# A hybrid encoder block: the sixth products' weights of two more halves summed by VectorE, turned gate rows stored and turned at other steps

## The chip, the core and the metric

The kernel runs on one core of a Trainium2 chip. Four engines compute: TensorE multiplies matrices (PE in the profile; PEld is its loading of weights), VectorE (DVE) and ScalarE (ACT) work on elements, GpSimd (POOL) here mostly issues DMA transfers. SyncE (SP) issues most of the others. Sixteen DMA engines carry all transfers of the core. The metric is the time of one execution in microseconds (us), the median of several runs; lower is better.

## The reference

One encoder layer on a sequence of 256 tokens of width 2048, all in float32. What matters here is that nearly all its work is products of the normalised input with wide weight matrices, and that some columns of `w_in` are gates:

```python
xn = rms_norm(x, norm_pre_w[l])
z = xn @ w_in[l]                    # 2048 x 13312
u_lru, g_lru, q, k, v, g_attn, m_lru, m_attn = jnp.split(z, split_at, axis=-1)
...
y_a = h.astype(x.dtype) * jax.nn.silu(g_lru)
...
y_b = windowed_gqa(q, k, v, attn_sink[l]) * jax.nn.silu(g_attn)
merged = (jax.nn.sigmoid(m_lru) * (y_a @ w_proj_a[l])
          + jax.nn.sigmoid(m_attn) * (y_b @ w_proj_b[l]))
x = x + rms_norm(merged @ w_out[l], norm_post_w[l])
```

## The kernel before

**Weights in two parts.** TensorE multiplies in a reduced float format (float32r), so every weight tile is split into a high part, rounded by a cast on ScalarE (line 222), and a low part, the rest, subtracted on VectorE (line 224). TensorE then multiplies high and low parts (lines 256, 258, 278, 435). Each 1 MB of weights passes as two halves, so ScalarE and VectorE have one instruction of 128 x 1024 elements each for every half.

**Steps and ticks.** The order of all weight pieces is written out by hand in START, MERGE and OUT. A step is one piece: a "block" (128 columns, two ticks long; blocks come in pairs), a "quad" (two ticks), or a "part" (one tick) of a group that saves a product. `soon(f, d)` calls f d ticks later, `at(n, f)` at tick n, in the order of the program; each engine runs its own instructions in that order. `seconds` lists the ticks at which the second block of a pair begins. Weights are fetched three steps ahead into a ring of three buffers (`raw`), high parts are made two steps ahead, low parts one and a half.

**Groups of seven.** L, H, M, N, A and O each compute a 1024-column product by seven products instead of eight (class `Seven`). Their names in START are, for example, Hm3.1: group H, third product, second half of the rows. L, H, M and N are the halves that lie in START, the first stage; H is half of the attention gate, the others are merge gates. The left operands are sums of input blocks, and the right operands are sums of weight blocks that build up in cells: x holds W11, then adds the second block (m5), then the third (m6), then the fourth (m4); y holds W for m3, then adds one for m7. Cells have the names Hx0a, Hx0b, Hx1a, Hx1b (group, cell, row half, a or b) and the like for y. Each addition is a DMA that reads weights from memory and adds them to the cell (`load(..., add=True)`, line 195, issued by POOL; queue q0 software_dynamic). It can go out when the cell's former content has been split by ScalarE and VectorE. `Seven.fetch` issues it five steps ahead, unless the group's products stand in ADDED (line 68). In that case `split` adds the third product's cell y to x on VectorE right behind the low part of the third product (line 227), since the weights that the sixth product needs added are those that m3 has alone. Before the change N, A and O do so for m6.

**Turned gate rows.** Group H yields rows of the attention gate with tokens on partitions, four tiles of 128 x 512 (`hr`). `silu_rows` applies the sigmoid and the product, and later `turn` transposes them on TensorE (line 831, into a PSUM buffer `ht` of a pool of two, which blocks in pairs use too), copies the result back with ScalarE (line 832), and `store` writes it to memory (`parksga`, line 839, on SP's queue), 256 KB each. A turn is put at the first second block that begins more than two ticks behind the sigmoid.

**Buffers.** Nearly everything big lives in one pool of 45 buffers of 4 KB a partition (`units`): high and low parts, cells, gate rows, input, LRU tiles, tiles on their way to memory and back. A new tile takes the buffer that has been free the longest, and its first writer waits until the former tile's last reader is done, a DMA store among them. Tiles that leave early go to memory by `park` (line 863; `parkq` is a tile of queries, `parkya` one of the LRU branch).

Of the kernel before, what the change touches and what calls it, by code (L numbers as in the profile page):

```python
# [64 lines left out]
LRU = (-4, 0, 0, 0, 0, 0, 0, 0)  # L65
QUADS = {"u": ("w_in", U0), "v": ("w_in", V0), "p": ("w_proj_a", 0),
         "b": ("w_proj_b", 0), "o": ("w_out", 0)}
ADDED = {'A': {'m3': 'm6', 'm2': 'm4'}, 'O': {'m3': 'm6'}, 'N': {'m3': 'm6'}}
PAIRS = {"g": GL0, "h": GA0, "w": U0, "k": K0, "q": Q0}
SEVENS = {"L": ("w_in", ML0 + 1024), "M": ("w_in", ML0), "N": ("w_in", MA0), "A": ("w_in", MA0 + 1536), "H": ("w_in", GA0 + 1024), "O": ("w_out", 0)}  # L70

# [39 lines left out]
def body(ctx, tc, x, x0, xT, wall, wlru, pvec, npost, ident_d, mask_d, rope_d, out):  # L111
# [9 lines left out]
    def unit(name, dt=F32, shape=(P, 4, S)):  # L121
        return units.tile(list(shape), dt, tag="u", name=name)
# [4 lines left out]
    def banks(name, shape=(P, 2, 2, S)):  # L127
        return psum.tile(list(shape), F32, tag="mm", name=name, bufs=2)

    def half_unit(name, tag, dt=F32, bufs=2):  # L130
        return small.tile([P, 2, S], dt, tag=tag, name=name, bufs=bufs)
# [20 lines left out]
    now = [0]  # L152

    def ticks(i=None):
        return sum(1 if p[0] == "part" else 2 for p in plan[:len(steps) if i is None else i])

    def at(hs, fn):
        assert hs >= now[0], (hs, now[0])
        due.setdefault(hs, []).append(fn)
# [9 lines left out]
    seconds, hs, n = [], 0, 0  # L169
# [7 lines left out]
    def soon(fn, d=1):  # L177
        at(now[0] + d, fn)
# [11 lines left out]
    def load(cell, p, add=False):  # L190

        w = wall[row[content(p)]]
        for h in range(2):
            if add:
                nc.gpsimd.dma_start(flat(cell[h]), w[:, h * 1024:(h + 1) * 1024], accum_op=ALU.add)
            else:
                nc.sync.dma_start(flat(cell[h]), w[:, h * 1024:(h + 1) * 1024])
# [14 lines left out]
    def split(q, c=0, w=1024, cast=nc.scalar.copy, only=None):  # L212
# [10 lines left out]
        if only != "h":  # L223
            nc.vector.tensor_tensor(ls, raw, hs.bitcast(F32), ALU.subtract)  # L224
            if plan[i][0] == "part" and plan[i][2] in ADDED.get(plan[i][1], ()):
                x = flat(groups[plan[i][1]].cells["x", plan[i][3]][h])
# [137 lines left out]
    def x_sum(name, s, q):  # L364
        t = unit(name, F32R, (P, 4, 2, P))
        nc.sync.dma_start(t.rearrange("p a b c -> p a (b c)").bitcast(F32), away[q][:, SUMS.index(s)])
        return t

    class Seven:
# [22 lines left out]
        def fetch(self, p, lead):  # L392
            m, q = p[2:]
            fresh = ("m1", "m3") if self.sums is None else ()
            if self.sums is None:
                if lead == 4 and m in fresh:
                    self.start(self.where(m), q)
                if lead == 4 and SEVEN[m][0][0] == "s" and self.name in "NA":
                    self.kept[m, q] = x_sum(f"{self.name}{m}{q}", SEVEN[m][0], q)
            if lead == 5 and m in ("m5", "m6", "m7", "m4")[self.sums is not None:] and m not in ADDED.get(self.name, {}).values():  # L400
                load(self.cell(m, q), p, True)
# [394 lines left out]
    def combine(to, ps, other, sign):  # L796
        nc.vector.scalar_tensor_tensor(to, ps, float(sign), other, ALU.mult, ALU.add if sign > 0 else ALU.subtract)
# [17 lines left out]
    def silu_rows(g):  # L815

        def done(t, c, ps, other, sign):
            u = unit(f"hr{g}{c}{t}")
            f, y = flat(u)[:, 0:512], u[:, 2:4].rearrange("p a (b s) -> p (a b) s", b=2)
            rt = rtok[:, t:t + 1]  # L820

            def sigmoid(src):
                sg = flat(half_unit(f"hs{c}{t}", "p"))
                nc.scalar.activation(sg, src, AF.Sigmoid, scale=rt)
                soon(lambda: nc.vector.scalar_tensor_tensor(f, src, rt, sg, ALU.mult, ALU.mult))
                at(min(b for b in seconds if b > now[0] + 2), turn)

            def turn():
                pt = banks(f"ht{c}{t}", (P, 4, P))
                for j in range(4):  # L830
                    nc.tensor.transpose(pt[:, j], f[:, j * P:(j + 1) * P], ident)
                nc.scalar.copy(y, pt)
                soon(store, 5)

            def store():
                key = "sga", g + c
                if key not in parked:
                    parked[key] = dram.tile([P, 1024], F32, name=f"parksga{g + c}")
                nc.sync.dma_start(parked[key].rearrange("p (j s) -> p j s", j=4)[:, :, t * P:(t + 1) * P], y)

            if other is None:
                sigmoid(ps)
            else:
                combine(f, ps, other, sign)
                soon(lambda: sigmoid(f))
        return done
# [317 lines left out]
    b, n = ticks(), ticks(len(plan))  # L1164
# [159 lines left out]
```

## Time and profile before

| | |
|---|---|
| median of 3 runs | 885.68 us (883.79 to 886.96) |
| the profiled execution | 884.68 us, span 882.9 us |
| granted TensorE clock, mean | 0.996 |
| busy: PE, DVE, ACT | 862.4, 750.3, 657.3 us |
| DMA | 244.77 MB, mean 277 GB/s |
| group H on TensorE | about 248 to 358 us of the span |
| group M on TensorE | about 357 to 460 us |

How to read the lines below. Rows of waits are "engine, line, tile waited for: us in total, times, longest". Rows of the chain of waits are "start us, us, what". Rows of the timeline are "start us, us, engine, line, operation, out<-in, count", with the engine's idle time before it in brackets and what ended it. Rows of groups are "line, engine, operation, tiles, count: duration in ns min/median/max, first and last start". Rows of windows give, for a stretch of the span, busy us and instructions of PE, PEld, DVE, ACT, POOL, then the granted TensorE clock, the busy share of the DMA engines and GB/s. Rows of DMA issues are "out<-in, queue, operation, count, KB each, median us from issue to landing". L224 is line 224 of the kernel.

### The profile page before, as it was taken

To read this page: it belongs to the slowest core of one execution; us is meant where nothing else is said; L and a number is where in the kernel's file an instruction comes from. 1 tells how busy PE (TensorE), PEld (TensorE's weight loads), DVE (VectorE), ACT (ScalarE), POOL (GpSimd) and SP (SyncE) were. 2 spreads that over 40 slices of the span, in tenths; PEclk is the share of its full clock that TensorE was granted. 3 is DMA by queue.
4 is the path that set the end of the run, shared out by engine and by line. 5 is a ranking of instruction groups with operands and counts; after the bars stand their busy time and mean duration, and the time that the engine had idled before them with its cause. 6 is when DMAs were issued, how large, how long until landed. Compare 5 with 4: busy or idle time off the path is not lost.

```text
span 882.9 us, 12249 instructions
## 1 busy us (share of the span) xinstructions
PE 862.4 (98%) x4378; PEld 733.9 (83%) x4378; DVE 750.3 (85%) x999; ACT 657.3 (74%) x939; POOL 73.0 (8%) x105
## 2 busy tenths in 40 slices
PE   9999999999999979999999999999999999999996
PEld 8888888888888868788888888778888888788885
DVE  6998999898898869797897887897669778998886
ACT  7689698969879868987976779996558545665654
POOL 0000001022011200112100020000000100000200
PEclk9999999999999999999999999999999999999999
DMA  9757699999999985999989998798999987988982
GB/s 328 275 191 250 196 315 290 278 298 250 306 255 350 260 206 195 293 270 295 280 270 328 305 288 301 251 324 334 272 327 370 298 325 215 309 311 316 266 205 95
DMA packets 68045, 244.77 MB, mean 277 GB/s; under 512 B 6416, under 2 KB 24592, under 8 KB 53264
## 3 DMA queue, kind: packets, MB, share of 16 engines
q1 hardware_dynamic: 52480, 198.37, 61.4%
q0 software_dynamic: 11520, 41.95, 25.1%
q10 hardware_dynamic: 3984, 3.67, 1.3%
q8 instruction: 34, 0.56, 0.2%
q14 instruction: 27, 0.22, 0.1%
HBM read 223.52 MB, written 20.45 MB: 276 GB/s over the span
## 4 chain that ended last, share of the span: by engine, by line
PE 81%; DMA 5%; DVE 5%; issue 4%; ACT 2%; SPq 1%; ACTq 1%; POOLq 0%; DVEq 0%
PE q L258 6%; PE gl L258 6%; PE u L258 5%; PE Lm L435 4%; PE Nm L435 4%; PE Hm L435 4%; PE Am L435 3%; PE ga L258 3%; PE q L256 3%; PE gl L256 3%; PE Om L435 3%; PE Mm L435 3%; PE pb__7297 L278 2%; PE pa__5741 L278 2%; PE pa__5992 L278 2%
## 5 line engine op out<-in xcount | busy, mean ns | idle before, releaser
L224 DVE TENSOR_TENSOR wl<-raw,wh 128x1024 fp32r<-128x1024 f32 (+1 forms) x240 | 285.2, 1201 | 53.1 <-ACT wh L222 38.6
L222 ACT CAST wh<-raw 128x1024 fp32r<-128x1024 f32 (+1 forms) x239 | 241.1, 1035 | 60.9 <-DMA raw<-wall_dram 31.1
L258 PE MATMUL gl<-xs,wh 128*128 128x512 f32 x256 | 64.8, 397 | 0.0
L258 PE MATMUL q<-xs,wh 128*128 128x512 f32 x256 | 63.9, 392 | 0.0
L258 PEld LDWEIGHTS gl<-xs,wh 128*128 128x128 f32 x256 | 48.1, 193 | 9.4
L258 PEld LDWEIGHTS q<-xs,wh 128*128 128x128 f32 x256 | 46.8, 188 | 9.0
L258 PE MATMUL u<-xs,wh 128*128 128x512 f32 x192 | 47.6, 391 | 0.0
L258 PEld LDWEIGHTS u<-xs,wh 128*128 128x128 f32 x192 | 35.1, 188 | 6.7
L256 PE MATMUL gl<-xs,wl 128*128 128x256 f32 x256 | 34.3, 285 | 5.1 <-DVE wl L224 5.1
L256 PEld LDWEIGHTS gl<-xs,wl 128*128 128x128 f32 x256 | 33.1, 191 | 7.0 <-DVE wl L224 5.7
L256 PEld LDWEIGHTS q<-xs,wl 128*128 128x128 f32 x256 | 33.0, 191 | 1.3
L256 PE MATMUL q<-xs,wl 128*128 128x256 f32 x256 | 33.5, 283 | 0.0
L258 PE MATMUL ga<-xs,wh 128*128 128x512 f32 x128 | 31.8, 391 | 0.0
L258 PEld LDWEIGHTS ga<-xs,wh 128*128 128x128 f32 x128 | 23.3, 189 | 4.3
L256 PEld LDWEIGHTS u<-xs,wl 128*128 128x128 f32 x192 | 24.7, 191 | 0.9
L256 PE MATMUL u<-xs,wl 128*128 128x256 f32 x192 | 25.1, 283 | 0.0
L686 DVE SCALAR_TENSOR_TENSOR uu<-upad,pv,uu 128x256 f32<-128x256 f32 x48 | 23.1, 482 | 1.7
L943 DVE CUSTOM_DVE_ANT_0 p<-sc,table,pv 128x256 f32<-128x256 f32 x32 | 16.0, 538 | 4.5 <-PE sc L233 4.5
L709 ACT ACTIVATE gr<-gate,pv 128x256 f32<-128x256 f32 x32 | 15.2, 475 | 5.9 <-DMA parkya<-sg 5.1
L231 PE MATMUL gate<-ul,lwh 128*128 128x256 f32 x64 | 18.2, 284 | 0.5 <-ACT gi L710 0.5
L949 ACT ACTIVATE p<-p,nm 128x256 f32<-128x256 f32 x32 | 16.0, 501 | 3.1 <-DVE nm L944 3.1
L233 PE MATMUL gate<-ul,lwl 128*128 128x256 f32 x64 | 18.1, 283 | 0.0
(567 smaller groups left out, 2230.9 us busy)
## 6 DMA issues: line engine op xcount, KB each, us to landing
raw<-wall_dram SPq DMA_DIRECT2D x115, 1024.0 KB, 7.8
lraw<-wlru_dram SPq DMA_DIRECT2D x8, 512.0 KB, 7.5
away<-xx SPq DMA_DIRECT2D x8, 512.0 KB, 8.3
Nm<-away SPq DMA_DIRECT2D x8, 512.0 KB, 9.5
turn<-pt SPq DMA_DIRECT2D x32, 128.0 KB, 6.0
pl<-turn SPq DMA_DIRECT2D x8, 512.0 KB, 6.8
Am<-away SPq DMA_DIRECT2D x8, 512.0 KB, 7.5
raw<-wall_dram SPq DMA_DIRECT2D x8, 256.0 KB, 5.1
```

Of the source, the lines that this page charges most:

```text
L222: cast(hs, raw)
L224: nc.vector.tensor_tensor(ls, raw, hs.bitcast(F32), ALU.subtract)
L231: nc.tensor.matmul(ps, wh, xh, start=start, stop=False, skip_group_check=more)
L233: nc.tensor.matmul(ps, wl, xh, start=False, stop=stop, skip_group_check=more)
L256: nc.tensor.matmul(ps[:, 1], wl[:, sl], a[:, 0], start=False, stop=False)
L258: nc.tensor.matmul(ps, wh[:, sl], a, start=k == 0, stop=k == KT - 1)
L278: nc.tensor.matmul(got[t], a[:, i], (wl if low else wh)[:, sl], start=k + low + i == 0, stop=low == 1 and k == KT - 1)
L435: nc.tensor.matmul(self.ps[b], a[i], (wl if low else wh)[:, sl], start=fresh and j + low + i == 0, stop=last and j + low == 2, skip_group_ ...
L686: nc.vector.scalar_tensor_tensor(u, up[:, j, tap:tap + S], cw[:, tap:tap + 1], u, ALU.mult, ALU.add)
L709: nc.scalar.activation(v["gr"][:, 2 * d + j], ps[:, 0], AF.Sigmoid, bias=pv[:, PV_BR + b:PV_BR + b + 1])
L943: nc.vector.tensor_tensor_reduce(p[:, t], sc[:, t], table["mask"][:, t], rtok_sc[:, t:t + 1], sk, ALU.add, ALU.max, m[:, t:t + 1])
L949: nc.scalar.activation(p[:, t], p[:, t], AF.Exp, bias=nm[:, t:t + 1], accum_out=dn[:, t:t + 1])
```

## The change

Groups H and M are entered in ADDED, so the second addition of their x cells, the one for the sixth product, is made by VectorE (line 227) and no longer by a DMA. Of the four halves of the first stage only L keeps the DMA. In `silu_rows` a turn is put at the first second block that begins more than four ticks behind the sigmoid, no longer two, and the store comes two ticks behind the turn, no longer five.

```diff
-ADDED = {'A': {'m3': 'm6', 'm2': 'm4'}, 'O': {'m3': 'm6'}, 'N': {'m3': 'm6'}}
+ADDED = {'A': {'m3': 'm6', 'm2': 'm4'}, 'O': {'m3': 'm6'}, 'N': {'m3': 'm6'}, 'H': {'m3': 'm6'}, 'M': {'m3': 'm6'}}
...
                 soon(lambda: nc.vector.scalar_tensor_tensor(f, src, rt, sg, ALU.mult, ALU.mult))
-                at(min(b for b in seconds if b > now[0] + 2), turn)
+                at(min(b for b in seconds if b > now[0] + 4), turn)
...
                 nc.scalar.copy(y, pt)
-                soon(store, 5)
+                soon(store, 2)
```

## The prediction

> **What bounds the kernel now.** I read the page first, then the waits of TensorE and VectorE, then the chain and the windows of the stage that the change touches.
>
> ```profile
> span 882.9 us, 12249 instructions
> PE 862.4 (98%) x4378; PEld 733.9 (83%) x4378; DVE 750.3 (85%) x999; ACT 657.3 (74%) x939; POOL 73.0 (8%) x105
> q0 software_dynamic: 11520, 41.95, 25.1%
> ```
>
> TensorE is the bound, with 20.5 us of idle time in all. The summing loads, the only work of queue q0, hold the 16 DMA engines for a quarter of the span. So a gain can only be idle TensorE time or a lowered clock that ends.
>
> ```profile
> PE gl L256 <- DVE wl L224: 5.1, 2, 3.9
> ...
> PE ht L831 <- ACT hr L832: 1.7, 1, 1.7
> ...
> PE Mm L435 <- DVE wl L224: 0.7, 1, 0.7
> ```
> ```profile
> DVE wl L224 <- DMA parksga<-hr: 10.0, 1, 10.0
> DVE wl L224 <- DMA parkq<-q0f: 5.6, 1, 5.6
> ```
>
> Three of TensorE's waits lie in the stage of groups H and M, 7.5 us together. Behind two of them stands VectorE, idle itself, because the buffer for its next low part was still being stored to memory. The chain shows the places:
>
> ```profile
> 303.69 12.96 DMA parksga<-hr
> ...
> 316.77 1.24 DVE wl L224
> ...
> 319.46 3.23 PE gl L258 x8
> ...
> 330.55 1.84 PE gl L258 x8
> ...
> 392.88 17.98 DMA parkq<-q0f
> ```
> ```profile
> 300.00:310.00 10.00, 10.00 (x55) 8.60 (x54) 6.61 (x8) 9.02 (x14) 2.45 (x5) 1.00 1.05 284
> 310.00:320.00 10.00, 6.08 (x33) 5.23 (x32) 3.20 (x4) 7.23 (x10) 0.46 (x1) 0.95 0.92 240
> 320.00:330.00 10.00, 8.85 (x40) 7.23 (x40) 9.75 (x14) 5.67 (x7) 1.29 (x2) 0.88 0.78 193
> ```
>
> A 256 KB store of a turned row took 12.96 us and a 512 KB one 17.98 us, with the DMA engines full (share 1.05). After the first stall the granted clock falls to 0.95 and 0.88: the same eight matmuls took 3.23 us there and 1.84 us later, so 1.4 us go on top. The H stall with its clock is worth 5.1 + 1.4 = 6.5 us.
>
> [...]
>
> **Part 1: eight summing loads leave POOL's queue.** Each group loses four of 512 KB.
>
> ```profile
> 273.89 0.86 POOL L195 DMA_DIRECT2D Hx0a<-wall_dram  x1 [18.48 <-DVE wl L224]
> ...
> 286.30 0.87 POOL L195 DMA_DIRECT2D Hx1b<-wall_dram  x1 [1.38 <-DVE wl L224]
> ...
> 398.05 0.86 POOL L195 DMA_DIRECT2D Mx1b<-wall_dram  x1 [2.03 <-DVE wl L224]
> ```
> ```profile
> raw<-wall_dram SPq DMA_DIRECT2D x115, 1024.0 KB, 7.8
> parksga<-hr SPq DMA_DIRECT2D x4, 256.0 KB, 9.1
> Hx1b<-wall_dram POOLq DMA_DIRECT2D x3, 512.0 KB, 11.0
> ```
>
> 41.95 MB are 80 loads of 0.524 MB, so one holds all engines for 25.1% x 882.9 / 80 = 2.8 us, and four free 11 us ahead of each late store. In H the last of the four is issued at 286.30, 17 us ahead of the store at 303.69; in M the last comes at 398.05, while the store is under way. How fast the H store becomes isn't shown; it lies between 12.96 us, as now, and 5.1 us, the median of the page's 256 KB loads:
>
> ```profile
> raw<-wall_dram SPq DMA_DIRECT2D x8, 256.0 KB, 5.1
> ```
>
> That is a landing between 308.8 and 316.7. I take the median of the four stores of turned rows, 9.1 us: 312.8.
>
> **Part 2: eight adds on VectorE.** An add of this shape exists in group N; its row, and the stretch in which H's four will stand (behind the low parts of Hy0a, Hy0b, Hy1a, Hy1b):
>
> ```profile
> L227 DVE TENSOR_TENSOR Nx0a<-Nx0a,Ny0a x1: 1219/1219/1219, 497.7 to 497.7; 128x1024 f32<-128x1024 f32 x1
> ```
> ```profile
> 289.81 1.22 DVE L224 TENSOR_TENSOR wl<-Hy0a,wh 128x1024 fp32r<-128x1024 f32 x1
> ...
> 297.11 1.22 DVE L224 TENSOR_TENSOR wl<-Hy1b,wh 128x1024 fp32r<-128x1024 f32 x1 [0.71 <-ACT wh L222]
> 298.25 2.50 DVE L224 TENSOR_TENSOR wl<-raw,wh 128x1024 fp32r<-128x1024 f32 x2
> ...
> 305.52 1.22 DVE L224 TENSOR_TENSOR wl<-raw,wh 128x1024 fp32r<-128x1024 f32 x1
> ...
> 328.06 1.22 DVE L224 TENSOR_TENSOR wl<-raw,wh 128x1024 fp32r<-128x1024 f32 x1
> ```
> ```profile
> 301.98 0.62 PE L435 MATMUL Hm<-wl,xx 128*128 128x512 f32 x2
> ...
> 304.73 2.07 PE L256 MATMUL u<-xs,wl 128*128 128x256 f32 x16
> ...
> 313.02 1.11 PE L256 MATMUL gl<-xs,wl 128*128 128x256 f32 x8
> ...
> 329.33 1.22 PE L256 MATMUL gl<-xs,wl 128*128 128x256 f32 x8 [1.15 <-DVE wl L224]
> ```
>
> Back to back such instructions start 1.14 us apart (297.11 and 298.25), so four cost 4.6 us and all eight 9.1 us. Following them through H: three adds stand ahead of Hy1b's low part, 3.4 us, of which its 0.71 us wait absorbs a part. It ends at 298.33 + 2.7 = 301.0; TensorE reads it at 301.98. With the fourth add the shift is 3.85 us. The next pair of low parts ends by 300.75 + 3.85 = 304.6; its second half is read eight matmuls behind 304.73, at 305.7. The part at 305.52 ends at 310.6 instead of 306.7. There VectorE waited 10.0 us for the store before; now it can go on at once if the buffer is free, and is in time if it starts by 312.7, since eight matmuls from 313.02 lead to 314.0 and the part takes 1.23. The store lands at about that moment. So H's adds lie in the 10.0 us wait, and the 3.9 us stall ends. If that cover were gone, they would cost 4.6 us.
>
> What is late next: the part that ended at 329.28. VectorE now passes 316.77 up to 6.2 us sooner and ends this one at 323.1; TensorE, freed of 6.5 us, asks for it at 322.8. A wait of about 0.3 us stays. H gives 6.5 - 0.3 = 6.2 us, with bounds of 0 (store as late as now) and 6.5.
>
> In M two adds stand ahead of the part that waited 5.6 us for the stored queries and two behind it. The store at 392.88 competed with four sums that are gone; without their 11 us it lands near 400, and VectorE comes by at about 407 instead of 405 (when its wait began). The 0.7 us stall ends; if the store stayed late, the last two adds would add up to 2.3 us. The remaining sums of both groups (into the y cells) now wait for the add that reads the cell, 1 to 4 us longer on POOL's queue; behind them are only the fourth products' sums, and ScalarE waits for these many steps later.
>
> **Part 3: stores three ticks sooner, last turn one block later.**
>
> ```profile
> 346.71 2.80 SPq L210 DMA_DIRECT2D raw<-wall_dram  x2
> 350.52 0.53 SPq L839 DMA_DIRECT2D parksga<-hr  x1
> ```
> ```profile
> 364.12 1.05 ACT L222 CAST wh<-raw 128x1024 fp32r<-128x1024 f32 x1
> ...
> 377.20 0.59 ACT L624 COPY q0f<-q 128x512 f32<-128x512 f32 x1 [2.63 <-PE q L258]
> ```
> ```profile
> 370.90 0.66 PE L831 MATMUL ht<-ident,hr 128*128 128x128 f32 x4 [1.67 <-ACT hr L832]
> ```
>
> By the plan's ticks the four turns fall due at 100, 113, 120, 120 before and 100, 113, 120, 127 after; the stores at 105, 118, 125, 125 and at 102, 115, 122, 129. The first store gains nothing: no load stands between ticks 102 and 105 in SP's queue, and it goes out when ScalarE's copy is done. The second moves ahead of two weight loads and, waiting for the copy, holds them until about 351.1, the first by 4.3 us. With 7.8 us to land it is there at 359, and ScalarE reads it at 364.12: nothing, but 4.3 us if that cover were gone. The third passes one load that waits for its own buffer: nothing.
>
> The fourth turn no longer asks for a PSUM buffer that the third still holds: the wait of 1.7 us goes. Its four transposes and ScalarE's copy move, none is added. The work on ScalarE behind the stall waits for TensorE's q pair (377.20), so it moves up with it, and I count the 1.7 us in full; bounds 0 and 1.7. Its store now goes out near 392, ahead of one weight load and the stored queries on SP's queue, and its buffer is held four ticks longer: nothing while the DMA engines have room, otherwise the third rival.
>
> **The sum.** 6.2 + 1.7 + 0.7 = 8.6 us off. The profiled execution took 884.68 us (span 882.9); 876.1 follows. The median of the three runs, 885.68, is 1.0 above it, so I forecast 877.1 us.
>
> **The rivals.**
> 1. The H store stays late. For it: the removed sums had 17 us until the store was issued, and take 11.0 us to land, so they were gone by then; sums into the y cells still compete. Against: what they displaced was pushed into the store's time, with the engines full. Only M and the turn give: 2.4 us, 883.3 us.
> [...]
> 2. VectorE becomes the bound in H.
> ```profile
> 270.00:350.00 80.00, 74.92 (x402) 64.69 (x400) 68.23 (x80) 65.69 (x92) 10.59 (x14) 0.98 0.84 235
> ```
> With 4.6 us more its 68.23 become 72.8, against TensorE's 74.92 - 1.4 = 73.5: no room for any other wait. If VectorE loses another 4 us to waits for ScalarE, H gives 2.2 and the time is 881.1 us. Against: it may start the stretch with its present lead.
> 3. Slower: the fourth row's buffer becomes the late one. Stored near 392 in front of M's weights, it may take as long as the stored queries do now, 17.98 us, to 410; the next low part to get it is due near 399. VectorE then stands 11 us, TensorE, about 4 us ahead of need, 7; with 1.4 us of clock, the last two adds (2.3) uncovered and the 0.7 not gained the loss against the forecast is 11.4, so 888.5 us. It ends above before once the store takes over about 15 us. Against: the four sums that slowed that stretch are gone.
>
> **How the numbers follow.** Forecast 0.56, rival 1 0.16, rival 2 0.12, rival 3 0.16. A measurement tells 0.3% (2.7 us) from no change. Faster: forecast 0.55, rival 2 0.10, rival 1 0.05, together 0.70; within 0.3%: 0.14, mostly rival 1; slower: 0.16. The range: 873.5 is the forecast less 3.6, for small gaps of the stage that I didn't price; 887 takes in rivals 1 and 2 and the milder half of 3. The forecast's own range is 874.5 to 880.
>
> **What would show it.** Waits of VectorE: no 10.0 for parksga and no 5.6 for parkq. Waits of TensorE: gl 5.1, ht 1.7, Mm 0.7 gone or under 1. Windows 310 to 330: clock 1.00. VectorE 9 us busier, 72 sums on q0. I am wrong if a new wait on a store appears between 390 and 420, or gl stays at 5.

## The result and the profile after

| | before | after |
|---|---|---|
| median of 8 runs | 885.60 us (882.89 to 888.53) | 879.86 us (877.86 to 883.66) |
| ratio to before, 95% interval | | 0.9943 (0.9925 to 0.9961) |
| the profiled execution | 884.68 us, span 882.9 us | 877.86 us, span 876.1 us |

The kernel became faster by 0.57%, about 5 us (3.5 to 6.6 by the interval); 8.6 us had been forecast. The profiled execution of after is the fastest of its eight runs, so the 6.8 us between the two spans say a little too much.

The top of the page after:

```profile
span 876.1 us, 12242 instructions
PE 861.9 (98%) x4378; PEld 734.1 (84%) x4378; DVE 758.6 (87%) x1007; ACT 657.4 (75%) x939; POOL 66.0 (8%) x97
q0 software_dynamic: 10368, 37.75, 22.7%
```

Eight additions more on VectorE (999 to 1007 instructions, 8.3 us of work) and eight issues less on POOL are there as the diff says, with 72 instead of 80 sums on queue q0. TensorE's work is the same, 861.9 us, so the gain is idle time and clock. The waits of TensorE after that lie in the stage of H and M are down to one row, but for one of 0.2 us:

```profile
PE Mm L435 <- DVE wl L224: 2.0, 1, 2.0
```

The rows gl (5.1) and ht (1.7) of before have gone, and Mm went from 0.7 to 2.0. The windows, with the granted clock third from the right:

```profile
310.00:320.00 10.00, 10.00 (x54) 8.57 (x53) 9.76 (x14) 6.60 (x9) 2.31 (x3) 1.00 1.06 284
320.00:330.00 10.00, 9.76 (x55) 8.14 (x54) 8.59 (x10) 9.96 (x13) 0.00 (x0) 1.00 0.68 172
...
380.00:390.00 10.00, 7.98 (x38) 6.46 (x38) 9.93 (x15) 8.02 (x13) 0.00 (x0) 0.83 0.46 120
```

In H (310 to 330) TensorE is full but for 0.24 us and the clock is 1.00, where before had 6.08 and 8.85 us of work at 0.95 and 0.88. In M there is a new hole at 380 to 390: 2.0 us of idle time and a clock of 0.83, with the DMA engines half empty (share 0.46).

So far this looks like the forecast with a blot in M. The chain and the timeline say that H was mended in another way than forecast. First the store of H's first turned row and the stored queries, in the chain and among the DMA issues of after:

```profile
303.25 13.19 DMA parksga<-hr
```
```profile
parkq<-q0f SPq DMA_DIRECT2D x1, 512.0 KB, 9.9
```

The store in H takes 13.19 us, not less than the 12.96 of before, and lands at 316.4 as late as then. The stored queries, 17.98 us before, take 9.9. And in H somebody still waits for the late store, in the timeline of ScalarE after:

```profile
316.52 1.06 ACT L222 CAST wh<-raw 128x1024 fp32r<-128x1024 f32 x1 [3.35 <-DMA parksga<-hr]
```

The tile that received the row's buffer is no longer a low part of VectorE (316.77 in the chain of before) but a high part of ScalarE, which had 3.35 us to lose there: TensorE's windows show almost nothing of it. Which tile gets which buffer is settled when the program is built, by the order of all its tiles' first and last uses. By that order the row's buffer went to the low part of the second half of g12.0 before and goes to the high part of the first half of g12.1 after. The additions read the cells y and x later than their splits do, and so shift the order in which buffers are released. The buffer of the stored queries, by contrast, goes to the same tile in both kernels, and in all the variants below that have 45 buffers: the low part of the first half of Mm3.1, which VectorE fills.

### The profile page after: what moved, and what is told of

Read it like the earlier page. It is cut to its first block, busy times and chain, and to the rows that moved or that the text cites. A ratio compares the mean times of both kernels' runs of the same rounds, so it can differ in the third digit from the quotient of the medians.

```text
span 876.1 us, 12242 instructions
## 1 busy us (share of the span) xinstructions
PE 861.9 (98%) x4378; PEld 734.1 (84%) x4378; DVE 758.6 (87%) x1007; ACT 657.4 (75%) x939; POOL 66.0 (8%) x97
## 4 chain that ended last, share of the span: by engine, by line
PE 84%; DVE 6%; issue 4%; DMA 3%; ACT 1%; ACTq 1%; POOLq 0%; SPq 0%; DVEq 0%
PE q L258 6%; PE gl L258 6%; PE u L258 5%; PE Lm L435 4%; PE Nm L435 4%; PE Hm L435 4%; PE Am L435 3%; PE ga L258 3%; PE q L256 3%; PE Mm L435 3%; PE Om L435 3%; PE gl L256 3%; PE u_ps L581 3%; DVE wl L224 3%; PE pb__7297 L278 3%
## 5 line engine op out<-in xcount | busy, mean ns | idle before, releaser
L258 PE MATMUL gl<-xs,wh 128*128 128x512 f32 x256 | 64.9, 398 | 0.0
L258 PE MATMUL q<-xs,wh 128*128 128x512 f32 x256 | 63.9, 392 | 0.0
L258 PEld LDWEIGHTS gl<-xs,wh 128*128 128x128 f32 x256 | 47.8, 192 | 9.3
L258 PEld LDWEIGHTS q<-xs,wh 128*128 128x128 f32 x256 | 46.8, 188 | 9.0
L258 PE MATMUL u<-xs,wh 128*128 128x512 f32 x192 | 47.6, 392 | 0.0
L258 PEld LDWEIGHTS u<-xs,wh 128*128 128x128 f32 x192 | 35.1, 188 | 6.7
L256 PEld LDWEIGHTS gl<-xs,wl 128*128 128x128 f32 x256 | 33.2, 192 | 1.7 <-DVE wl L224 0.2
L256 PEld LDWEIGHTS q<-xs,wl 128*128 128x128 f32 x256 | 33.0, 191 | 1.3
L256 PE MATMUL gl<-xs,wl 128*128 128x256 f32 x256 | 33.8, 284 | 0.0
L256 PE MATMUL q<-xs,wl 128*128 128x256 f32 x256 | 33.5, 283 | 0.0
L258 PE MATMUL ga<-xs,wh 128*128 128x512 f32 x128 | 31.8, 391 | 0.0
L258 PEld LDWEIGHTS ga<-xs,wh 128*128 128x128 f32 x128 | 23.3, 189 | 4.3
L256 PEld LDWEIGHTS u<-xs,wl 128*128 128x128 f32 x192 | 24.7, 191 | 0.9
L256 PE MATMUL u<-xs,wl 128*128 128x256 f32 x192 | 25.1, 283 | 0.0
```

Of the source, the lines that this page charges most:

```text
L256: nc.tensor.matmul(ps[:, 1], wl[:, sl], a[:, 0], start=False, stop=False)
L258: nc.tensor.matmul(ps, wh[:, sl], a, start=k == 0, stop=k == KT - 1)
```

## The experiments

Two theories stood against each other for H. **Transfer**: with four sums less the store and the loads around it run freer, as the prediction has it. **Hand-out**: the additions moved the last uses of the cells, another tile got the late buffer, and that the sums left the DMA engines does nothing for H. Ratios are to the kernel before on the same chip, with their 95% intervals.

**The two parts alone.** Adds only:

```diff
-ADDED = {'A': {'m3': 'm6', 'm2': 'm4'}, 'O': {'m3': 'm6'}, 'N': {'m3': 'm6'}}
+ADDED = {'A': {'m3': 'm6', 'm2': 'm4'}, 'O': {'m3': 'm6'}, 'N': {'m3': 'm6'}, 'H': {'m3': 'm6'}, 'M': {'m3': 'm6'}}
```

> Groups H and M get their sums from VectorE; turns and stores as before. Buffer theory (what ended the H stall is that another tile takes the first turned row's buffer; in this program it is a high part of the second half of g12, as in the changed kernel): VectorE doesn't wait for parksga, TensorE's gl wait under 1 us, though the 256 KB store still takes 12 to 14 us. Transfer theory (the removed sums made the store land sooner): no wait either, but the store takes under 10 us. Both: the ht wait of about 1.7 us is back, and the wait ahead of Mm is under 1 us, since TensorE comes later; 878 to 882 us.

Measured: 0.9931 (0.9902 to 0.9960), the whole gain. Turns and stores only:

```diff
-                at(min(b for b in seconds if b > now[0] + 2), turn)
+                at(min(b for b in seconds if b > now[0] + 4), turn)
...
-                soon(store, 5)
+                soon(store, 2)
```

> Stores sooner and the last turn later, sums by DMA as before. Both theories: the gl wait of about 5 us with VectorE waiting 10 us for parksga stays (the same low part takes the buffer as before), ht gone. If the 1.7 us of ht are really gained the time is 883 to 884 us; if VectorE's chain in M gives them back, a wait of about 2 us ahead of Mm or gl appears and the time stays at 885 to 886 us.

Measured: 0.9998 (0.9971 to 1.0026). Rows of the waits of adds only, then of turns only:

```profile
PE ht L831 <- ACT hr L832: 2.4, 1, 2.4
PE gl L256 <- DVE wl L224: 1.2, 2, 0.7
ACT wh L222 <- DMA parksga<-hr: 4.4, 1, 4.4
```
```profile
PE gl L256 <- DVE wl L224: 5.0, 3, 3.3
PE Mm L435 <- DVE wl L224: 1.3, 2, 0.8
DVE wl L224 <- DMA parksga<-hr: 16.1, 2, 9.4
```

With the adds it is ScalarE that waits for the row's store, which took 14.2 us, and gl falls from 5.1 to 1.2; with the turns alone it is VectorE, and gl stays at 5.0. The second part removes the wait of 1.7 us for ht and still gains nothing.

**Sums gone, adds left out.** In the changed kernel the eight additions of H and M were left out, so that neither VectorE nor a DMA adds the sixth products' weights there, and the sixth and fourth products are computed with cells that lack them:

```diff
-            if plan[i][0] == "part" and plan[i][2] in ADDED.get(plan[i][1], ()):
+            if plan[i][0] == "part" and plan[i][1] not in "HM" and plan[i][2] in ADDED.get(plan[i][1], ()):
```

> The changed kernel without VectorE's eight adds: the weights that H's and M's sixth products need added are left out altogether. In this program the low part of g12's first block takes the first turned row's buffer, as in the kernel before. Buffer theory: VectorE waits some 8 to 10 us for parksga again and TensorE 3 to 5 us for gl, although eight sums are gone and nothing was put in their place: 879 to 884 us, no faster than the changed kernel. Transfer theory: the store takes under 10 us, no gl wait over 1 us, and without the adds the time is 873 to 877 us.

Measured: 0.9945 (0.9915 to 0.9975). Its chain and its waits:

```profile
303.81 11.66 DMA parksga<-hr
...
315.60 1.22 DVE L224 TENSOR_TENSOR wl<-raw,wh 128x1024 fp32r<-128x1024 f32 x1 [8.73 <-DMA parksga<-hr]
```
```profile
PE gl L256 <- DVE wl L224: 5.5, 4, 2.6
DVE wl L224 <- DMA parksga<-hr: 8.7, 1, 8.7
```

This is the case against the transfer theory in H. Four sums are gone and nothing was put in their place, yet the store takes 11.66 us, VectorE gets the late buffer again and waits 8.7 us, and TensorE loses 5.5 us at gl. What this kernel gains lies elsewhere: the ht wait of 1.7 us is gone, and the clock stays at 1.00 in H, where before lost 1.4 us to it. Its ratio alone would have misled.

**VectorE's work alone.** In the kernel before, each low part of the third products of H and M is computed twice, as much added work as the adds, with all sums still by DMA:

```diff
+            if plan[i][0] == "part" and plan[i][1] in "HM" and plan[i][2] == "m3":
+                nc.vector.tensor_tensor(ls, raw, hs.bitcast(F32), ALU.subtract)
```

> The kernel before, with VectorE computing each low part of H's and M's third products twice (eight more instructions of the adds' length at the adds' places); all sums by DMA. In this program the low part of Hm6.1 takes the first turned row's buffer, one part later than before. Buffer theory: TensorE's gl wait falls under 1.5 us with all sums still on the DMA queue; M as before plus up to 2.3 us; 880 to 884 us. Transfer theory: the gl wait stays at 4 to 6 us and the time is 886 to 890 us.

Measured: 1.0056 (1.0031 to 1.0082), a miss for both theories' numbers. Its waits (by the two inserted lines, what was L256 and L435 is L258 and L437, and L226 is the second computation):

```profile
PE gl L258 <- DVE wl L224: 4.3, 3, 2.5
PE Mm L437 <- DVE wl L226: 3.5, 2, 2.2
DVE wl L224 <- DMA parksga<-hr: 6.1, 1, 6.1
```

The buffer moved on, to the low part of Hx1a, which is a tile of VectorE again. It is not enough that another tile gets the buffer: it must be one whose engine has time, as ScalarE had and VectorE, with its doubled work, had not.

**The hand-out alone.** In the kernel before, GpSimd writes four elements into the first turned row four ticks behind its store, after which nobody reads them. The row's buffer so counts as in use for longer and is handed out later, to a high part of Hm7.0. All sums stay with the DMA and no addition is made:

```diff
                 nc.sync.dma_start(parked[key].rearrange("p (j s) -> p j s", j=4)[:, :, t * P:(t + 1) * P], y)
+                if c == 0 and t == 0:
+                    soon(lambda: nc.gpsimd.memset(u[:, 0, 0:4], 0.0), 4)
```

> The kernel before with one change: GpSimd writes four dead elements of the first turned row four ticks behind its store, so its buffer is handed out later (to a high part of the fourth products' neighbour, needed about 10 us later) and not to the low part of g12. All sums stay on the DMA queue, VectorE gets nothing more. If the hand-out of that buffer is the whole of the H stall: no wait of VectorE for parksga, TensorE's gl wait under 1 us, clock 1.00 between 310 and 330, and the time falls by 4 to 7 us to 879 to 882 us, as much as the adds gave. If the sums' transfers matter in H: gl stays above 3 us, 884 to 887 us.

Measured: 0.9932 (0.9908 to 0.9956), 879.02 us: as much as the whole change, by an instruction that computes nothing. Its waits, a row of ScalarE's timeline, chain and windows:

```profile
PE Mm L435 <- DVE wl L224: 1.8, 1, 1.8
PE ht L831 <- ACT hr L832: 1.7, 1, 1.7
...
PE gl L256 <- DVE wl L224: 0.4, 1, 0.4
DVE wl L224 <- DMA parkq<-q0f: 6.7, 1, 6.7
```
```profile
320.92 1.06 ACT L222 CAST wh<-Hy0b 128x1024 fp32r<-128x1024 f32 x1 [0.47 <-DMA parksga<-hr]
```
```profile
386.20 19.11 DMA parkq<-q0f
```
```profile
310.00:320.00 10.00, 10.00 (x53) 8.57 (x53) 9.25 (x13) 9.94 (x13) 1.87 (x3) 1.00 1.06 265
...
400.00:410.00 10.00, 8.18 (x31) 6.34 (x30) 4.57 (x5) 5.47 (x9) 1.74 (x2) 0.87 1.04 308
```

H is as clean as after the change: gl 0.4, clock 1.00, with the DMA engines just as full (1.06). The row's store was not faster: it took 16.9 us, against 12.96 before, and its buffer's new owner on ScalarE lost only 0.47 us to it. GpSimd's write itself begins at 315.43, right behind the issue of the last of H's sums in the stretch (314.89), so it held none of them back. What is left is M's stall on the stored queries (19.11 us) and the ht wait: the two things that the change treats apart from H.

**One group alone.** In the changed kernel, adds in H only, then in M only:

```diff
+ADDED = {'A': {'m3': 'm6', 'm2': 'm4'}, 'O': {'m3': 'm6'}, 'N': {'m3': 'm6'}, 'H': {'m3': 'm6'}}
```

> The changed kernel with adds in H alone; M's sums go back to DMA. H as in the changed kernel: no gl wait over 1 us. M: VectorE waits 4 to 6 us for the stored queries again and TensorE about 1 us ahead of Mm3.1, unless TensorE's wait ahead of Mm5 has eaten it. If H carries the gain: 879 to 882 us; if M does: 883 to 885 us.

```diff
+ADDED = {'A': {'m3': 'm6', 'm2': 'm4'}, 'O': {'m3': 'm6'}, 'N': {'m3': 'm6'}, 'M': {'m3': 'm6'}}
```

> The changed kernel with adds in M alone; H's sums go back to DMA, and the low part of g12 takes the first turned row's buffer again. The gl wait of 4 to 5 us stays, the wait for the stored queries is gone. If H carries the gain: 883 to 886 us; if M does: 880 to 882 us.

Measured: 0.9999 (0.9978 to 1.0020) with H's, 0.9974 (0.9953 to 0.9994) with M's. Waits of H's adds only, then of M's only:

```profile
PE Mm L435 <- DVE wl L224: 5.3, 3, 2.6
DVE wl L224 <- DMA parkq<-q0f: 6.8, 1, 6.8
ACT wh L222 <- DMA parksga<-hr: 5.4, 1, 5.4
```
```profile
PE gl L256 <- DVE wl L224: 5.5, 3, 4.4
DVE wl L224 <- DMA parksga<-hr: 10.5, 1, 10.5
```

With H's adds the buffer goes to ScalarE and the gl stall goes, but the time comes back in M. TensorE waits 5.3 us there: 2.6 us behind the stored queries, for which VectorE waits 6.8, and 2.7 us, in two waits, around the place where the changed kernel waits 2.0. With M's adds the queries' store no longer delays VectorE and H's stall stays. In the changed kernel the cure of H pays only together with M's adds. That is no rule: the kernel with the hold gains 0.7% with M's stall in place.

In M the transfer theory holds. The stored queries with the turns alone, and with M's adds put to them:

```profile
parkq<-q0f SPq DMA_DIRECT2D x1, 512.0 KB, 15.9
```
```profile
parkq<-q0f SPq DMA_DIRECT2D x1, 512.0 KB, 9.2
```

These two programs differ in M's adds alone, the stores go out at 394.94 and 394.70, and the buffer goes to the same tile. Unlike in H, a sum that was taken away had here still been under way with the store: in the kernel before the last of them was issued at 398.05.

**Four weight buffers in the ring** (the changed kernel with four `raw` buffers, and 43 general ones to make room). This was to tell whether the new wait in M hangs on the ring of weights:

```diff
-UNITS = 45
+UNITS = 43
...
-        t = ring.tile([P, 2, 1024], F32, tag="raw", name=f"raw{i}", bufs=3)
+        t = ring.tile([P, 2, 1024], F32, tag="raw", name=f"raw{i}", bufs=4)
```

> The changed kernel with four instead of three buffers for loaded weights and, to make room, 43 instead of 45 general buffers. If the wait of 2.0 us ahead of Mm5 and the lowered clock behind it come from the weight load that could go out only when VectorE had freed a buffer of the ring (issued at 364.14, landed 7.5 us later while ScalarE waited 3.1 us): the wait falls under 0.5 us, clock 1.00 in 380 to 390, and the time is 875 to 878 us if two general buffers fewer cost nothing. If VectorE's queue itself is what is late, the wait stays at 1.5 to 2.5 us; if the general buffers are short, new waits for buffers appear and the time is over 880 us.

Measured: 1.0047 (1.0027 to 1.0066). Its waits:

```profile
PE gl L256 <- DVE wl L224: 2.7, 3, 1.4
PE Hm L435 <- ACT wh L222: 1.9, 1, 1.9
PE Mm L435 <- DVE wl L224: 1.2, 2, 0.9
ACT wh L222 <- DMA parksga<-hr: 7.5, 1, 7.5
```

Two general buffers fewer bring new waits all over the stage, so the time says nothing of the ring. Mm fell from 2.0 to 1.2 only. Inconclusive.

**What beats both kernels.** The hold of the fifth experiment was joined with the parts that still had something to give: with M's adds (hold of four ticks), with H's and M's adds, and with M's adds and the change's turns and stores (hold of eight ticks). The last, against the kernel before:

```diff
+ADDED = {'A': {'m3': 'm6', 'm2': 'm4'}, 'O': {'m3': 'm6'}, 'N': {'m3': 'm6'}, 'M': {'m3': 'm6'}}
...
+                at(min(b for b in seconds if b > now[0] + 4), turn)
...
+                soon(store, 2)
...
+                if c == 0 and t == 0:
+                    soon(lambda: nc.gpsimd.memset(u[:, 0, 0:4], 0.0), 8)
```

> The kernel before with the first turned row's buffer handed out later (the four dead elements of GpSimd) and M's sums on VectorE; H's sums by DMA, turns and stores as before. If the H stall is the hand-out and the second late store (the queries) is cured by taking M's sums off the DMA queue: no gl wait over 1 us, no wait of VectorE for the queries, the wait ahead of Mm under 1 us, ht about 1.7 to 2.5 us: 876 to 879 us, faster than the changed kernel and than the held kernel alone. If M's sums don't matter: as the held kernel, 878 to 880 us.

> As the run before it, with H's sums on VectorE too. If H's adds bring nothing but another order of hand-out, they cost up to 4.6 us of VectorE's time here and the time is 878 to 881 us, not below the run with M's adds alone; if freeing the queue in H is worth something of its own, it is 874 to 877 us.

> M's adds and the held buffer with the changed turns and stores. If the last turn's move only shifts TensorE's wait from ht to the wait ahead of Mm5: 876 to 880 us, within 1.5 us of the run without the move, with ht gone and about 2 us ahead of Mm or gl. If the move is a gain once H is cured: 873 to 876 us.

| | median | ratio (95% interval) |
|---|---|---|
| hold and M's adds | 875.90 us | 0.9906 (0.9884 to 0.9928) |
| hold and both groups' adds | 877.94 us | 0.9920 (0.9903 to 0.9937) |
| hold, M's adds, turns and stores | 874.99 us | 0.9891 (0.9875 to 0.9907) |

Once the hand-out is settled by the hold, H's adds bring nothing that can be seen: with them the kernel is, if anything, slower, though the intervals overlap. The third version is the fastest of all, with an interval that lies wholly below the change's own (0.9925 to 0.9961); against the first, the intervals overlap, so that the moved turn gains something here is not shown by the time. Its waits say that it is not lost here: ht is gone, and no wait over 0.4 us has come in M in its place. Two windows of it, and its stored queries:

```profile
310.00:320.00 10.00, 10.00 (x53) 8.61 (x52) 8.88 (x12) 9.94 (x13) 1.87 (x3) 1.00 1.06 271
...
380.00:390.00 10.00, 9.62 (x57) 8.10 (x56) 10.00 (x13) 9.54 (x14) 0.00 (x0) 1.00 0.63 181
```
```profile
parkq<-q0f SPq DMA_DIRECT2D x1, 512.0 KB, 9.0
```

Both holes of the stage are closed but for 0.4 us, at a clock of 1.00.

## Why the prediction was right and where it was wrong

**Direction, bound and prices.** The change was faster for the reason that the views of before gave: VectorE's waits for buffers under store were TensorE's stalls, and they went. The price of the adds was right. Two rows of after, of the additions by group and of VectorE's timeline:

```profile
L227 DVE TENSOR_TENSOR Hx0a<-Hx0a,Hy0a x1: 1214/1214/1214, 290.4 to 290.4; 128x1024 f32<-128x1024 f32 x1
```
```profile
301.40 2.35 DVE L224 TENSOR_TENSOR wl<-raw,wh 128x1024 fp32r<-128x1024 f32 x2
...
308.31 2.35 DVE L224 TENSOR_TENSOR wl<-raw,wh 128x1024 fp32r<-128x1024 f32 x2
```

An addition takes 1214 ns (1219 taken) and the pair behind them ends at 303.75 (304.6 forecast). The part at 305.52 before, the first half of g12.0, now begins at 308.31 and ends at about 309.5 (310.6 forecast), and the second half, which had waited 10.0 us, follows at once and is done at 310.66. So the additions fit into what had been VectorE's wait.

**H: the size was right, the step was wrong.** The forecast gave 6.2 us, on the step that the store, rid of four sums, lands at 312.8 instead of 316.7. It landed at 316.4. The bound "0 (store as late as now)" came true and the gain came all the same, because the low part at which VectorE had waited got another buffer. That H's term came out is luck. I followed every instruction of VectorE through the stretch and never asked whether the shift would change who inherits the row's buffer. The first rival named the right fact for the store, "gone by then", and gave H nothing for it; it fell on the same gap. With four sums fewer the store still took 13.19 us, against 12.96; what kept it as long is not shown. The forecast priced the 0.3 us of wait left in H without any loss of clock, which was my estimate: after the change TensorE has no wait for gl there at all, and the clock is 1.00 in both windows. That H's gain is a matter of the hand-out is shown by the third and fifth experiments, one with the sums gone and the stall kept, one with the sums kept and the stall gone.

**M: right.** "Without their 11 us it lands near 400": the queries' store took 9.9 us instead of 17.98 and landed at 398, and VectorE no longer waits for it. The price was too low: 0.7 us is what M lost while H's stall still held it back. With H's stall gone and M's sums left in place, TensorE loses 1.8 us and clock there (fifth experiment) or 2.6 us (H's adds only). So M's part was worth more in the whole than its own row before said.

**The turn: this term of the sum failed.** I counted the 1.7 us in full, since ScalarE "moves up" with TensorE's q pair. ScalarE's timeline of after, and then the chain:

```profile
368.09 0.59 ACT L624 COPY q0f<-q 128x512 f32<-128x512 f32 x1 [0.94 <-PE q L258]
371.75 2.00 ACT L222 CAST wh<-raw 128x1024 fp32r<-128x1024 f32 x2 [3.07 <-DMA raw<-wall_dram]
```
```profile
364.14 7.53 DMA raw<-wall_dram
...
374.66 1.13 DVE wl L224
...
378.38 1.16 DVE wl L224
...
382.11 1.23 DVE wl L224
```

ScalarE did move up, to 368.09, and then stood 3.07 us before the next weights, whose load could only go out at 364.14, when VectorE released a buffer of the ring, and took 7.53 us. From there VectorE's low parts follow with other work in between, and the one that TensorE needs next begins at 382.11: the 2.0 us of Mm. The same place in the held kernel with M's adds, where the turn was not moved, in ScalarE's timeline:

```profile
371.43 0.59 ACT L624 COPY q0f<-q 128x512 f32<-128x512 f32 x1 [2.63 <-PE q L258]
371.91 2.00 ACT L222 CAST wh<-raw 128x1024 fp32r<-128x1024 f32 x2
```

There the copy comes 3.3 us later and the cast follows with no wait at 371.91, only 0.16 us behind the 371.75 of after (these two kernels differ in H's adds and the hold too). TensorE's 1.7 us were not removed but carried on to the next thing that it lacks, and came back as 2.0 with a clock of 0.83, an estimated 1.4 us more (8 us of work at 0.83). The adds alone show the other side: with the turn left in its place TensorE waits 2.4 us for ht and not at all for Mm, and the ratio is no worse (0.9931 against 0.9943). By the rows of the two profiled executions: 6.5 in H, 0.7 in M and 1.7 for ht, less 2.0 and 1.4, are 5.5 of the 6.8 us between them; the medians differ by 5.7.

The move is not lost everywhere. In the fastest version the same load is there about 1.9 us sooner (its cast begins at 369.87), and the 2.0 us do not appear. From the first low part behind that load to the start of the one that TensorE needs VectorE takes 9.2 us there (370.95 to 380.17) and 9.3 us after the change (372.84 to 382.11). So VectorE's work in between is the same, and it is the load's landing that decides the wait. It was issued only 0.5 us sooner there (363.66); why it then also landed faster is not shown, and the ring of four did not tell.

**The rivals.** VectorE as the bound of H did not come about: TensorE's windows in H are full. Nor did the late store of the fourth row, though its mechanism is real: with the turns alone and the sums still on their queue that store, issued at 392.44, took 14.1 us and VectorE waited 6.7 us for it, of which TensorE lost 0.8. The doubled low parts show that the fear was not idle: without what the change does for the DMA engines and the hand-out, the same work on VectorE costs time (1.0056).

## What to carry to other kernels

In a pool that hands buffers out in the order of their release, an edit far away can decide who inherits a buffer that is still being stored; before costing a transfer, look up which tile gets its buffer, which engine fills that tile, and how much time that engine has. A stall that is removed from an engine which others run ahead of is worth only the distance to the next thing it lacks: follow the next load, the next low part and the next store to that point before counting it in full. And test the mechanism apart from the change: one late write of four dead elements gave 0.7%, as much as the whole edit with its 0.6%, and with it the parts that were really needed could be told from those that only came along.

## What the runs showed of the hardware

In these runs the granted clock did not follow the length of a wait alone. A wait of 2.0 us was followed by 0.83 (after), and one of 1.8 us by 0.87 (before with the hold), while one of 2.63 us in the kernel without additions was followed by 1.00. TensorE's timeline there and its window:

```profile
316.87 1.22 PE L256 MATMUL gl<-xs,wl 128*128 128x256 f32 x8 [2.63 <-DVE wl L224]
```
```profile
310.00:320.00 10.00, 7.37 (x41) 6.25 (x39) 4.37 (x5) 7.34 (x10) 0.88 (x1) 1.00 0.94 272
320.00:330.00 10.00, 7.54 (x40) 6.12 (x39) 9.76 (x14) 6.68 (x8) 0.87 (x1) 1.00 0.68 146
```

The wait of 3.9 us in the kernel before was followed by 0.88. So shorter waits than that one also came with a lowered clock here, and the 2.0 us of after cost an estimated 1.4 us more (8 us of work at 0.83).

In these runs a store's time said little about its size. The 256 KB of H's first row took 12.96 us before, 13.19 us with four sums fewer, 11.66 us with the additions left out too and 16.9 us with the hold, at a share of the DMA engines of 0.92 to 1.06 in the windows of these four kernels that begin at 310. The 512 KB of the stored queries took, with M's sums on their queue, 17.98 us before, 15.9 us with the turns alone, 19.1 us with the hold and 19.3 us with H's adds only; without M's sums they took 9.9 us after the change, 9.8 us with the additions left out, 9.2 us with M's adds only and 9.0 us in the fastest kernel.
